# Seven of 128 rows of a row maximum reduced through TensorE, ScalarE and GpSimd instead of VectorE, with 24 loads in place of 29

## The chip, the cores and the metric

One core of one Trainium2 chip runs the program. The metric is the device time of one execution in microseconds; lower is better. Both kernels give the reference's result. A profiled execution gives the span of the program on the core, which is about 1.8 us shorter than the time (kernel before: 163.4 us of 165.17).

## The reference

```python
x = np.random.randn(32, 512, 1024).astype(np.float32)
def reference(x):
    return np.max(x, axis=-1).astype(np.float32)
```

That is 16,384 rows of 1024 floats: 67.1 MB to read and 64 KB to write. Spread over 128 partitions there are 128 rows per partition, and "a row" below means one row in each of the 128 partitions, 512 KB.

## The kernel before

One queue (SyncE) loads several rows at a time into a ring of 45 rows per partition; VectorE reduces each load with one instruction. The loads get smaller towards the end, so that little is left to do when the last one lands; the very last row comes in two halves.

```python
BLOCKS = [
    [14, 13, 12, 11, 9, 8, 8, 7, 6, 5, 5, 4, 4, 3, 3],
    [2, 2, 2, 1, 1, 1, 1, 1, 1, 1, 1, 1],
]
RING = 45
# ... (cut)
        for n in loads:
            if at + n > RING:
                at = 0
            xc = ring[:, at:at + n, :]
            nc.sync.dma_start(out=xc, in_=xb[:, b:b + n, :])
            reduce = nc.vector.reduce_max(out=res[:, first + b:first + b + n], in_=xc, axis=X)
            at += n
            b += n
# ... (cut)
    nc.sync.dma_start(out=half, in_=xb[:, b, :H])
    nc.sync.dma_start(out=tail[:, PAD:], in_=xb[:, b, H:])
    nc.vector.reduce_max(out=tail[:, PAD - 1:PAD], in_=half, axis=X)
    nc.vector.reduce_max(out=res[:, I - 1:], in_=tail[:, PAD - 1:], axis=X)
```

## Time and profile before

| | before |
|---|---|
| time, median (lowest to highest) | 165.0 us (164.85 to 165.12) |
| span of the profiled execution | 163.4 us |
| VectorE busy | 139.0 us, 85% |
| load queue, share of 16 DMA engines' time | 96.6% |
| loads | 27 and two halves |
| last half row landed (landing records) | 159.75 us |

Two shares near the top do not say which of the two, loads or VectorE, sets the end. For that one compares two times: when the last load has landed, and when VectorE gets to it. The prediction below does this with the profile's lines. The trace records 16 landings for each load (496 for the 29 loads and the two stores), taken here as one for each of the page's 16 DMA engines. For each of the five loads that VectorE waited for, its reduction starts 0.02 to 0.03 us behind the last of the 16 (first load: the last landing at 20.29 us, the reduction at 20.31).

### The profile page before, as it was taken

To read this page: it belongs to the slowest core of one execution; us is meant where nothing else is said; L and a number is where in the kernel's file an instruction comes from. 1 tells how busy PE (TensorE), PEld (TensorE's weight loads), DVE (VectorE), ACT (ScalarE), POOL (GpSimd) and SP (SyncE) were. 2 spreads that over 40 slices of the span, in tenths; PEclk is the share of its full clock that TensorE was granted. 3 is DMA by queue.
4 is the path that set the end of the run, shared out by engine and by line. 5 is a ranking of instruction groups with operands and counts; after the bars stand their busy time and mean duration, and the time that the engine had idled before them with its cause. 6 is when DMAs were issued, how large, how long until landed. Compare 5 with 4: busy or idle time off the path is not lost.

```text
span 163.4 us, 117 instructions
## 1 busy us (share of the span) xinstructions
DVE 139.0 (85%) x29; POOL 0.2 (0%) x4
## 2 busy tenths in 40 slices
DVE  0000099989998999999999999999999999999994
POOL 0000000000000000000000000000000000000000
DMA  6999999999989989999989999999999999999990
GB/s 225 449 449 449 433 417 417 417 401 529 433 385 430 452 386 432 433 433 441 457 385 481 401 442 422 409 438 421 446 409 425 437 410 422 427 407 409 409 355 16
DMA packets 4464, 67.18 MB, mean 411 GB/s; under 512 B 752, under 2 KB 752, under 8 KB 2160
## 3 DMA queue, kind: packets, MB, share of 16 engines
q1 hardware_dynamic: 4176, 67.11, 96.6%
q10 hardware_dynamic: 288, 0.07, 0.2%
HBM read 67.11 MB, written 0.07 MB: 411 GB/s over the span
## 4 chain that ended last, share of the span: by engine, by line
DVE 49%; DMA 48%; SPq 1%; issue 0%
DMA ring<-in_x_dram 48%; DVE res L58 48%; SPq L57 1%; DVE res L70 0%; DVE tail L69 0%
## 5 line engine op out<-in xcount | busy, mean ns | idle before, releaser
L58 DVE TENSOR_REDUCE res<-ring 128x1 f32<-128x1024 f32 (+12 forms) x27 | 137.7, 5165 | 22.1 <-DMA ring<-in_x_dram 22.1
L70 DVE TENSOR_REDUCE res<-tail 128x1 f32<-128x513 f32 x1 | 0.7, 686 | 0.0
L69 DVE TENSOR_REDUCE tail<-ring 128x1 f32<-128x512 f32 x1 | 0.7, 682 | 0.0
L90 POOL MEMSET const-bfloat16-1.0<- 128x1 bf16 x1 | 0.1, 102 | 0.0
L90 POOL MEMSET const-uint8-127<- 128x1 uint8 x1 | 0.1, 102 | 0.0
L90 POOL MEMSET const-float32-0.0<- 128x1 f32 x1 | 0.1, 99 | 0.2 <-issue 0.2
L90 POOL MEMSET const-float32-1.0<- 128x1 f32 x1 | 0.1, 99 | 0.0
## 6 DMA issues: line engine op xcount, KB each, us to landing
ring<-in_x_dram SPq DMA_DIRECT2D x2, 4096.0 KB, 25.6
ring<-in_x_dram SPq DMA_DIRECT2D x1, 7168.0 KB, 19.6
ring<-in_x_dram SPq DMA_DIRECT2D x1, 6656.0 KB, 34.9
ring<-in_x_dram SPq DMA_DIRECT2D x1, 6144.0 KB, 48.9
ring<-in_x_dram SPq DMA_DIRECT2D x1, 5632.0 KB, 28.5
ring<-in_x_dram SPq DMA_DIRECT2D x2, 2560.0 KB, 38.4
ring<-in_x_dram SPq DMA_DIRECT2D x1, 4608.0 KB, 24.7
ring<-in_x_dram SPq DMA_DIRECT2D x9, 512.0 KB, 13.8
```

The lines of the kernel that those rows point to most:

```text
L57: nc.sync.dma_start(out=xc, in_=xb[:, b:b + n, :])
L58: reduce = nc.vector.reduce_max(out=res[:, first + b:first + b + n], in_=xc, axis=X)
L69: nc.vector.reduce_max(out=tail[:, PAD - 1:PAD], in_=half, axis=X)
L70: nc.vector.reduce_max(out=res[:, I - 1:], in_=tail[:, PAD - 1:], axis=X)
L90: nc = _bacc.Bacc("TRN2", target_bir_lowering=False, num_devices=1)
```

## The change

The intent is to relieve VectorE. Seven rows, out of the loads numbered 6, 7 and 9 (counted from 0), take a side path: TensorE turns a row in eight 128x128 transposes, ScalarE copies it from PSUM, where the kernel has TensorE write it, GpSimd takes the maximum over partitions, eight small transposes bring the maxima back, and VectorE merges the eight values of each row. With VectorE relieved, the loads can be larger and fewer. The identity that TensorE needs is made by VectorE.

```diff
 BLOCKS = [
-    [14, 13, 12, 11, 9, 8, 8, 7, 6, 5, 5, 4, 4, 3, 3],
+    [15, 15, 15, 15, 14, 11, 11, 8, 4, 4],
     [2, 2, 2, 1, 1, 1, 1, 1, 1, 1, 1, 1],
 ]
+TENSOR = {
+    6: [("turn", 6, 0), ("turn", 6, 1), ("back", 6, 0), ("back", 6, 1)],
+    7: [("turn", 7, 0), ("turn", 7, 1), ("turn", 7, 2), ("back", 7, 0), ("back", 7, 1)],
+    9: [("turn", 9, 0), ("turn", 9, 1), ("back", 7, 2), ("back", 9, 0), ("back", 9, 1)],
+}
+BY_GPSIMD = {6: 2, 7: 3, 9: 2}
+MERGE = {8: 6, 12: 7, 16: 9}
 # ... (cut: pools, the identity)
+    def turn(j, k):
+        rows, cols = tiles[j]
+        ps = psum.tile([P, D], F32)
+        for c in range(C):
+            in_turn("PE", nc.tensor.transpose(
+                out=ps[:, c * P:(c + 1) * P],
+                in_=rows[:, k, c * P:(c + 1) * P],
+                identity=ident,
+            ))
+        sb = turned.tile([P, D], F32)
+        nc.scalar.copy(out=sb, in_=ps)
+        top = allr.tile([P, D], F32)
+        nc.gpsimd.partition_all_reduce(top, sb, P, bass_isa.ReduceOp.max)
+        tops[j, k] = top
+
+    def back(j, k):
+        if j not in backs:
+            fetched = psmall.tile([P, BY_GPSIMD[j], C], F32)
+            backs[j] = fetched
+        for c in range(C):
+            in_turn("PE", nc.tensor.transpose(
+                out=backs[j][:, k, c:c + 1],
+                in_=tops[j, k][0:1, c * P:(c + 1) * P],
+                identity=ident[0:1, 0:1],
+            ))
 # ... (cut)
-            reduce = nc.vector.reduce_max(out=res[:, first + b:first + b + n], in_=xc, axis=X)
+            m = BY_GPSIMD.get(j, 0)
+            tiles[j] = xc[:, n - m:, :], cols[:, n - m:]
+            for what, i, k in TENSOR.get(j, []):
+                (turn if what == "turn" else back)(i, k)
+            reduce = in_turn("DVE", nc.vector.reduce_max(
+                out=cols[:, :n - m], in_=xc[:, :n - m, :], axis=X))
+            if j in MERGE:
+                i = MERGE[j]
+                in_turn("DVE", nc.vector.reduce_max(out=tiles[i][1], in_=backs[i], axis=X))
```

More of the change, by code (lines that the diff above doesn't have):

```diff
@@ L4 @@
 import concourse.tile as tile
-from concourse import bass_utils, mybir
+from concourse import bass_isa, bass_utils, mybir
 from concourse._compat import with_exitstack
@@ L17 @@
 RING = 45
+TENSOR = {
[5 more added lines that the diff above has]
+MERGE = {8: 6, 12: 7, 16: 9}
+NOSYNC = mybir.DependencyInfo(mybir.DependencyClass.NoSync, mybir.DependencyReason.DATA)
 SYNC = mybir.DependencyInfo(mybir.DependencyClass.Sync, mybir.DependencyReason.DATA)
@@ L30 @@
     X = mybir.AxisListType.X
+    ALU = mybir.AluOpType
     xf = x.flatten_outer_dims()
@@ L34 @@
     H = D // 2
+    C = D // P
     I = N // P
@@ L38 @@
     once = ctx.enter_context(tc.tile_pool(name="once", bufs=1))
+    turned = ctx.enter_context(tc.tile_pool(name="turned", bufs=2))
+    allr = ctx.enter_context(tc.tile_pool(name="allr", bufs=2))
+    psum = ctx.enter_context(tc.tile_pool(name="psum", bufs=3, space=bass.MemoryType.PSUM))
+    psmall = ctx.enter_context(tc.tile_pool(name="psmall", bufs=2, space=bass.MemoryType.PSUM))
     ring = once.tile([P, RING, D], F32)
@@ L43, with in_turn @@
     tail = once.tile([P, PAD + H], F32)
-    at = first = 0
+    latest = {}
+    def in_turn(engine, inst):
+        if engine in latest:
+            tc.add_manual_dep(inst.ins, latest[engine].ins.name, NOSYNC, reason="in turn")
+        latest[engine] = inst
+        return inst
+    ident = once.tile([P, P], F32)
+    colno = once.tile([P, P], F32)
+    rowno = once.tile([P, 32], F32)
+    in_turn("DVE", nc.vector.memset(ident, 1.0))
+    in_turn("DVE", nc.vector.memset(rowno, 0.0))
+    in_turn("DVE", nc.vector.tensor_tensor_scan(
+        out=colno, data0=ident, data1=ident, initial=-1.0, op0=ALU.add, op1=ALU.mult))
+    in_turn("DVE", nc.vector.transpose(out=rowno, in_=colno[:, :32]))
+    for q in range(1, P // 32):
+        part = rowno[q * 32:(q + 1) * 32, 0:1]
+        in_turn("DVE", nc.vector.tensor_scalar(
+            out=part, in0=part, scalar1=float(q * 32), scalar2=None, op0=ALU.add))
+    in_turn("DVE", nc.vector.tensor_scalar(
+        out=ident, in0=colno, scalar1=rowno[:, 0:1], scalar2=None, op0=ALU.is_equal))
+    tiles = {}
+    tops = {}
+    backs = {}
+    def turn(j, k):
[22 more added lines that the diff above has]
+            ))
+    at = first = j = 0
     views = []
@@ L57 @@
             nc.sync.dma_start(out=xc, in_=xb[:, b:b + n, :])
-            reduce = nc.vector.reduce_max(out=res[:, first + b:first + b + n], in_=xc, axis=X)
+            cols = res[:, first + b:first + b + n]
+            m = BY_GPSIMD.get(j, 0)
[7 more added lines that the diff above has]
+                in_turn("DVE", nc.vector.reduce_max(out=tiles[i][1], in_=backs[i], axis=X))
             at += n
             b += n
+            j += 1
         first += S
@@ L68 @@
     nc.sync.dma_start(out=tail[:, PAD:], in_=xb[:, b, H:])
-    nc.vector.reduce_max(out=tail[:, PAD - 1:PAD], in_=half, axis=X)
-    nc.vector.reduce_max(out=res[:, I - 1:], in_=tail[:, PAD - 1:], axis=X)
+    in_turn("DVE", nc.vector.reduce_max(out=tail[:, PAD - 1:PAD], in_=half, axis=X))
+    in_turn("DVE", nc.vector.reduce_max(out=res[:, I - 1:], in_=tail[:, PAD - 1:], axis=X))
     store = nc.scalar.dma_start(out=views[0][0], in_=views[0][1])
```

## The prediction

> **What bounds the kernel now.** I read the page of the profile first, then the timeline of VectorE and of the load queue, then the groups by form, then the table of stretches. From the page:
>
> ```profile
> span 163.4 us, 117 instructions
> ...
> DVE 139.0 (85%) x29; POOL 0.2 (0%) x4
> ...
> q1 hardware_dynamic: 4176, 67.11, 96.6%
> ...
> DVE 49%; DMA 48%; SPq 1%; issue 0%
> ```
>
> VectorE is busy for 85% of the span, but the load queue fills 96.6% of it. The chain that ended last is half one, half the other, so the question is which of them the end belongs to. The timeline (start, duration, engine, line) answers it:
>
> ```profile
> 20.31 15.09 DVE L58 TENSOR_REDUCE res<-ring 128x14 f32<-128x14336 f32 x1 [20.31 <-DMA ring<-in_x_dram]
> 36.05 14.02 DVE L58 TENSOR_REDUCE res<-ring 128x13 f32<-128x13312 f32 x1 [0.65 <-DMA ring<-in_x_dram]
> 50.58 12.95 DVE L58 TENSOR_REDUCE res<-ring 128x12 f32<-128x12288 f32 x1 [0.51 <-DMA ring<-in_x_dram]
> ...
> 94.27 65.48 DVE L58 TENSOR_REDUCE res<-ring 128x8 f32<-128x8192 f32 x21 [0.21 <-DMA ring<-in_x_dram]
> ...
> 150.77 0.33 SPq L68 DMA_DIRECT2D tail<-in_x_dram  x1
> 159.66 0.68 DVE L69 TENSOR_REDUCE tail<-ring 128x1 f32<-128x512 f32 x1
> ...
> 160.38 0.69 DVE L70 TENSOR_REDUCE res<-tail 128x1 f32<-128x513 f32 x1
> 161.10 0.34 ACTq L75 DMA_DIRECT2D out_dram<-res  x1
> ```
>
> VectorE has no gap from 94.27 us on, so it looks like the bound. The last load says otherwise:
>
> ```profile
> tail<-in_x_dram SPq DMA_DIRECT2D x1, 256.0 KB, 9.0
> ```
>
> Issued at 150.77 and landed 9.0 us later, the last half row is there at 159.8 (159.75 in the landing records). VectorE begins to reduce it at 160.38, only 0.6 us late. So the loads own the end; VectorE adds 0.6 us of backlog and its last 0.7 us reduction.
>
> **Cost of a load.** The first three lines of the timeline start at landings: 13 rows take 36.05 - 20.31 = 15.74 us, 12 rows 14.53 us, so about 1.21 us a row (a row is 512 KB). Single rows are slower, as the table of stretches shows (last column GB/s):
>
> ```profile
> 1.60:50.00 48.40, 29.04 (x2) 0.00 (x0) 1.00 1.02 435
> 148.20:157.10 8.90, 8.90 (x8) 0.00 (x0) 1.00 1.03 411
> ```
>
> 524,288 bytes at 411 GB/s are 1.276 us. Both fit 1.206 us a row plus 0.07 us a load (12 rows: 14.54).
>
> **Cost of a reduction.** By form:
>
> ```profile
> L58 DVE TENSOR_REDUCE res<-ring 128x14 f32<-128x14336 f32 x1 | 15.1, 15086 | 20.3 <-DMA ring<-in_x_dram 20.3
> L58 DVE TENSOR_REDUCE res<-ring 128x13 f32<-128x13312 f32 x1 | 14.0, 14019 | 0.7 <-DMA ring<-in_x_dram 0.7
> ```
>
> 15,086 - 14,019 = 1,067 ns a row. The unbroken 65.48 us hold 60 rows in 21 instructions: 60 x 1.067 = 64.0, leaving 0.07 us an instruction. A single row thus costs 1.13 us against 1.28 us of its load: VectorE catches up 0.15 us with each.
>
> [...]
>
> **The change, part by part.**
>
> 1. *Fewer, larger loads.* 29 loads become 24 for the same 128 rows: 5 x 0.07 = 0.35 us less. Last landing about 159.4 us instead of 159.75.
>
> 2. *A later start.* The first load has 15 rows, not 14: VectorE starts 1.2 us later, at 21.5. This is harmless, as parts 3 and 4 show.
>
> 3. *Ring.* Three loads of 15 fill its 45 rows. The fourth needs the first one's reduction, at 21.5 + 16.1 = 37.6, while loads two and three keep the queue busy until 21.5 + 2 x 18.16 = 57.8. The fifth is issued at 39.7 + 16.1 = 55.8, the sixth at 57.8 + 16.1 = 74, before load four lands at 76. So at least one whole load is queued behind the running one at every refill, and no gap comes. The rows sent round VectorE lie in slots never loaded again, so a slow GpSimd doesn't hold up a load.
>
> 4. *VectorE loses seven rows,* 7 x 1.067 = 7.5 us. These can't come off the end, which the loads own. With landings from part 1, VectorE waits for nearly every load; its lag at the end of the two-row loads is one reduction. Landings: load 6 (eleven rows) 119.6, load 7 129.4, load 8 134.3, load 9 139.2, the last two-row load 146.6, the ninth single row 158.1. Three merges of 16 or 24 values are added (estimate 0.15 us each). From 148.8 us: merge 0.15, four single rows 4.5, merge 0.15, ready at about 153.6; five more rows end at 159.3 (the last waits for 158.1), first half 159.9, second half 160.6. Before it was 161.07: **0.5 us less**.
>
> 5. *The side path.* A turn is eight transposes[...], a copy of 1024 elements[...], then GpSimd's t, then eight small transposes back[...].[...] TensorE's order is part of this: the turns of load 7 stand behind the way back of load 6, so there GpSimd idles for one turn.
>
>    I do not know t. I chose about 3 us because the program's order makes sense there: both ways back of load 6 stand before load 7's turns, which costs nothing only if two reductions take no longer than load 7 needs to land, and the third way back of load 7 stands behind load 9's turns, as if it were expected about then.
>
> 6. *Preparation.* The identity takes seven or eight small VectorE instructions in the 21 us it idles anyway: no cost. [...]a few more instructions are fetched. I allow 0.2 us, on the load queue or at the ends.
>
> Sum: -0.5 (VectorE's end, the 0.35 of fewer loads contained in it) + 0.2 = -0.3 in the fitting case. To that comes about 0.2 us as the share of the cases in which the side path is somewhat late. 165.0 - 0.3 + 0.2 = 164.9; I place the single figure at **164.7**, nearer the fitting case.
>
> **Rivals.** *A wait for GpSimd takes the place of the wait for loads:* [...]the end follows the seven reductions at 7 us for each us of t. Nothing in the profile measures it; against it stands the order of the program[...].[...] *Expected gain through freed VectorE:* who takes 85% busy and the unbroken 65 us for the bound expects 7 us less, 158. The landing of the last half row at 159.75 speaks against it: the loads alone do not end before 159.4. *Other traffic delays the loads:* all 16 DMA engines are full (96.6%), so every byte of [...]instructions fetched on one of them puts off the end by its own time[...]. *Same ends:* all fits, 164.3 to 164.7.
>
> **Range and chances.** The fitting case and its small delays cover 164.2 to 165.2. A moderate delay[...] reaches 167. Range 164.0 to 167.2. A gain of 2% (below 161.7) would need the loads to end 3 us earlier[...]: 0.01. A loss of 2% (above 168.3)[...]: 0.11. Within 2%: 0.88.
>
> **What would show it.** Right: the last half row lands at 159.4 +- 0.3; VectorE busy about 132 us with idle time <- DMA spread over nearly all loads; final reduction starts within 0.1 us of the half before it; no VectorE wait <- TensorE at the merges. Wrong: a wait of VectorE <- PE before the second or third merge[...]; starts of GpSimd's reductions more than 4 us apart; landings of single rows over 1.28 us apart, or later than 159.8 (then traffic was added); load-queue share falling well below 96% (then the ring starved).

Where a cut is marked, the text had times for a turn, a copy and a way back of the side path, the time table and the limits for t (GpSimd's time for one reduction) made from them, a library of GpSimd and an example of its size, a limit for the rate of the loads. The sum came to -0.5 + 0.2 = -0.3 us in the fitting case, to 164.9 us with 0.2 us added for a late side path, and the single figure was put at 164.7. That the loads themselves can gain little rests on the queue's 96.6% and on the 435 GB/s of the first stretch.

## The result, and the profile after

The changed kernel takes 165.83 us (165.78 to 165.94, four runs) against 165.0 us before. The ratio is 1.0051, with a 95% interval of 1.0034 to 1.0069. Ratios here are the mean time of one kernel's fast runs over that of the other's fast runs of the same rounds, so they are not quite the ratio of the medians.

The page of the changed kernel, same parts as shown of before, with two more lines from the parts on DMA and on the costliest groups:

```profile
span 164.0 us, 368 instructions
...
q1 hardware_dynamic: 3456, 67.11, 95.9%
...
q8 instruction: 1, 0.02, 0.0%
...
DMA 69%; DVE 28%; SPq 1%; issue 0%
...
L106 POOL PARTITION_ALL_REDUCE top<-sb x7 | 22.5, 3269 | 127.2 <-ACT sb L104 127.2
L104 ACT COPY sb<-ps 128x1024 f32<-128x1024 f32 x7 | 7.1, 1013 | 136.2 <-PE ps L98 134.5
```

The chain that ended last has gone over to the loads: 69% DMA, where before it was shared half and half. VectorE really was relieved: it is busy for 134.0 us, before 139.0. GpSimd's reduction takes 3.27 us by its record; in the timeline (start, duration) two of them in a row take 6.43 us, so they follow each other every 3.2 us:

```profile
119.39 3.65 PE L98 MATMUL ps<-ident,ring 128*128 128x128 f32 x16 [119.39 <-DMA ring<-in_x_dram]
...
122.47 6.43 POOL L106 PARTITION_ALL_REDUCE top<-sb  x2 [122.05 <-ACT sb L104]
...
150.14 1.01 PE L115 MATMUL fetched<-ident,top 1*128 1x1 f32 x8 [2.20 <-POOL top L106]
...
153.81 0.16 DVE L143 TENSOR_REDUCE res<-fetched 128x2 f32<-128x16 f32 x1
...
160.20 0.68 DVE L155 TENSOR_REDUCE tail<-ring 128x1 f32<-128x512 f32 x1
160.91 0.69 DVE L156 TENSOR_REDUCE res<-tail 128x1 f32<-128x513 f32 x1
```

The last maxima are back at 151.2 us, and VectorE merges them at 153.8 without an idle mark in brackets: nobody waits for the side path. Yet the final reduction starts at 160.91, 0.5 us later than before (160.38).

Why the loads are late shows in one line of the page, easily overlooked: "q8 instruction: 1", one transfer of 0.02 MB of instructions in the middle of the stream. The record of this transfer says one packet of 16,384 bytes, start 146.31 us, 1,079 ns. The 16 landing times of the loads around it (from the landing records, us, sorted; the middle ones cut) tell what it did:

```
third two-row load     145.89 145.90 145.92 ... 146.15 146.16 146.21 146.22
first single row       147.16 147.18 147.19 ... 147.43 147.46 147.49 148.81
second single row      148.43 148.44 148.47 ... 148.69 148.71 148.76 150.10
last half row          158.73 158.74 158.76 ... 158.97 159.00 159.03 160.32
```

Up to 146.2 us the 16 landings lie within 0.4 us for every load. From the first single row on, one of them is 1.3 us behind the other 15, and it stays so to the end. (The trace does not name the engine of the transfer; that one engine has the transfer and the late landings is read from the times.) On the other 15 the loads are not late; the last half row would be complete at 159.03 (159.15 in the run with one transpose back of eight, which has no transfer), but it is complete at 160.32.

### The profile page after: what moved, and what is told of

The parts are those of the page before. It is cut to its first block, busy times and chain, and to the rows that moved or that the text cites. A ratio compares the mean times of both kernels' runs of the same rounds, so it can differ in the third digit from the quotient of the medians.

```text
span 164.0 us, 368 instructions
## 1 busy us (share of the span) xinstructions
PE 19.1 (12%) x112; PEld 17.6 (11%) x112; DVE 134.0 (82%) x35; ACT 8.4 (5%) x8; POOL 22.7 (14%) x11
## 3 DMA queue, kind: packets, MB, share of 16 engines
q1 hardware_dynamic: 3456, 67.11, 95.9%
## 4 chain that ended last, share of the span: by engine, by line
DMA 69%; DVE 28%; SPq 1%; issue 0%
DMA ring<-in_x_dram 69%; DVE res L139 27%; SPq L133 1%; DVE res L156 0%; DVE tail L155 0%
## 5 line engine op out<-in xcount | busy, mean ns | idle before, releaser
L139 DVE TENSOR_REDUCE res<-ring 128x1 f32<-128x1024 f32 (+7 forms) x22 | 131.0, 5969 | 26.6 <-DMA ring<-in_x_dram 26.1
L106 POOL PARTITION_ALL_REDUCE top<-sb x7 | 22.5, 3269 | 127.2 <-ACT sb L104 127.2
L98 PE MATMUL ps<-ident,ring 128*128 128x128 f32 x56 | 12.6, 421 | 119.4 <-DMA ring<-in_x_dram 119.4
L98 PEld LDWEIGHTS ps<-ident,ring 128*128 128x128 f32 x56 | 11.5, 228 | 119.4 <-issue 119.4
L104 ACT COPY sb<-ps 128x1024 f32<-128x1024 f32 x7 | 7.1, 1013 | 136.2 <-PE ps L98 134.5
L115 PE MATMUL fetched<-ident,top 1*128 1x1 f32 x56 | 6.7, 236 | 12.7 <-POOL top L106 12.7
L115 PEld LDWEIGHTS fetched<-ident,top 1*128 1x128 f32 x56 | 6.1, 203 | 14.0 <-POOL top L106 13.7
L143 DVE TENSOR_REDUCE res<-fetched 128x2 f32<-128x16 f32 (+1 forms) x3 | 0.5, 166 | 0.0
## 6 DMA issues: line engine op xcount, KB each, us to landing
ring<-in_x_dram SPq DMA_DIRECT2D x9, 512.0 KB, 15.2
```

Source lines behind the costliest of these rows:

```text
L98: in_turn("PE", nc.tensor.transpose(out=ps[:, c * P:(c + 1) * P], in_=rows[:, k, c * P:(c + 1) * P], identity=ident,))
L104: nc.scalar.copy(out=sb, in_=ps)
L106: nc.gpsimd.partition_all_reduce(top, sb, P, bass_isa.ReduceOp.max)
L115: in_turn("PE", nc.tensor.transpose(out=backs[j][:, k, c:c + 1], in_=tops[j, k][0:1, c * P:(c + 1) * P], identity=ident[0:1, 0:1],))
L139: reduce = in_turn("DVE", nc.vector.reduce_max(out=cols[:, :n - m], in_=xc[:, :n - m, :], axis=X))
L143: in_turn("DVE", nc.vector.reduce_max(out=tiles[i][1], in_=backs[i], axis=X))
```

## The experiments

Theory A: with more instructions on TensorE, a block of them is fetched during the run, the 16,384 bytes of the record; it occupies one of the 16 DMA engines, which the loads fill to 95.9%, for 1.08 us, and every later load waits for that engine. Rivals: the larger loads themselves (B), VectorE as the bound (C), TensorE's, ScalarE's or GpSimd's reading and writing in SBUF, where the kernel has its ring (D), a library for GpSimd as the thing fetched (E).

| kernel | transposes | instruction transfer, start | last half row landed | time, median |
|---|---|---|---|---|
| before | 0 | none | 159.75 | 165.0 |
| before, seven rows left out | 0 | none | 159.47 | 164.89 |
| new loads, seven rows left out | 0 | none | 159.13 | 164.46 |
| changed, one transpose back of eight | 63 | none | 159.15 | 164.55 |
| changed | 112 | 146.31 | 160.32 | 165.83 |
| changed, no GpSimd | 112 | 144.44 | 160.48 | 166.01 |
| before + 112 idle transposes | 112 | 17.52 | 160.87 | 166.32 |
| before + 336 idle transposes | 336 | 17.43 and 31.12 | 160.83 | 166.29 |
| before + 80 idle transposes | 80 | none | 159.52 | 164.94 (one run) |
| before + 96 idle transposes | 96 | 163.65, after the span (163.3) | 159.48 | 165.04 (one run) |
| new loads, VectorE alone | 0 | none | 159.13 | 170.71 (one run) |
| four rows on the side path, 26 loads | 64 | none | 159.22 | 164.84 |
| changed, ways back in groups | 80 | none | 159.20 | 165.31 |
| the same, last merge later | 80 | none | 159.18 | 164.64 |

(The second, third and fourth columns are from the profiled execution of each, landings from the landing records. The profiled execution of the kernel before took 165.17 us, so its 159.75 is rather late: the three other profiles of the same loads without a transfer in the stream end at 159.47 to 159.52.)

**The side path taken away.** The seven rows are neither reduced nor sent; results are wrong in those columns.

```diff
-TENSOR = {6: [...], 7: [...], 9: [...]}
-MERGE = {8: 6, 12: 7, 16: 9}
+TENSOR = {}
+MERGE = {}
+    in_turn("DVE", nc.vector.memset(res, 0.0))      # in place of the identity
```

> The changed kernel's loads, with the seven rows left out altogether: no TensorE, no ScalarE copy, no GpSimd, no merge (wrong results in seven columns, on purpose). Theory A (the 16 KB instruction fetch on one DMA engine is what the change paid): no fetch in the DMA table, all 16 engines land together again, last half row at 159.3 us instead of 160.3, final reduction starts by 160.1, time 164.4 to 164.8. Theory B (the new loads themselves are the slower part, for instance the 15-row loads): last landing stays at 160.3, time 165.7 to 165.9. Theory C (the seven rows were the bound all along): time below 163.

Measured 164.46 us, ratio to before 0.9973 (0.9958 to 0.9988), last landing 159.13. So the new loads are not the slow part: with 24 of them the kernel is 0.45 us faster than before. Rivals B and C are out, the latter because even with seven rows for nothing the time does not go below 164.

**Fewer transposes back.** Everything stays but seven of the eight small transposes of each row (wrong results).

```diff
-            fetched = psmall.tile([P, BY_GPSIMD[j], C], F32)
+            fetched = psmall.tile([P, BY_GPSIMD[j], 1], F32)
-        for c in range(C):
+        for c in range(1):
```

> The changed kernel with one of the eight transposes back of each row (wrong results in seven columns, on purpose): 63 transposes instead of 112; GpSimd, ScalarE and VectorE do all they did. Theory A (fetch of TensorE's instructions): no 16 KB instruction transfer, last landing 159.3, time 164.5 to 164.9, 1 us less than the changed kernel. Rival D (GpSimd's or TensorE's reading of SBUF slows the loads): landing and time within 0.2 us of the changed kernel's 160.3 and 165.8. Rival E (the fetch belongs to GpSimd's library): the 16 KB transfer stays, and so does the time.

Measured 164.55 us, ratio 0.9978 (0.9961 to 0.9995). The page of this run has no line for an instruction queue, and the queue and timeline lines that answer to those of the changed kernel are:

```profile
span 162.8 us, 270 instructions
...
q1 hardware_dynamic: 3456, 67.11, 96.6%
q10 hardware_dynamic: 288, 0.07, 0.2%
HBM read 67.11 MB, written 0.07 MB: 413 GB/s over the span
...
L106 POOL PARTITION_ALL_REDUCE top<-sb x7 | 22.5, 3267 | 125.8 <-ACT sb L104 125.8
```

```profile
159.73 0.69 DVE L156 TENSOR_REDUCE res<-tail 128x1 f32<-128x513 f32 x1
```

GpSimd still does its seven reductions in 22.5 us, and the span is 1.2 us shorter. Rivals D and E do not fit: all of GpSimd's and ScalarE's work is there, and the loss is gone. Of TensorE's work 49 small transposes are missing, so its part of D is left to the runs with idle transposes below.

**GpSimd taken away, transposes kept.** The ways back read the turned row (wrong results).

```diff
-        top = allr.tile([P, D], F32)
-        nc.gpsimd.partition_all_reduce(top, sb, P, bass_isa.ReduceOp.max)
-        tops[j, k] = top
+        tops[j, k] = sb
```

> The changed kernel with the reduction over partitions left out: the transposes back read the turned row itself (wrong results, on purpose). All 112 transposes stay. Theory A: the 16 KB instruction transfer is still there, though perhaps earlier, one engine ends about 1.3 us after the others, time 165.6 to 165.9. Rivals D (GpSimd's traffic) and E (GpSimd's library): transfer gone or landing at 159.3, time 164.4 to 164.9.

Measured 166.01 us (165.82 to 166.25), 0.1 us over the range I had written, ratio 1.0068 (1.0053 to 1.0083). The transfer is there, at 144.44, 1.9 us earlier; TensorE does not wait for GpSimd here, for which it waited 12.7 us in the changed kernel. GpSimd's reduction is gone and the transfer is not, so the transfer is neither caused by GpSimd's work nor a library for it.

**The transposes put into the kernel before.** VectorE makes the identity as in the change, and TensorE turns a constant tile into PSUM at the start; nothing reads it, and the results are right.

```diff
+    for _ in range(14):
+        ps = psum.tile([P, D], F32)
+        for c in range(D // P):
+            nc.tensor.transpose(out=ps[:, c * P:(c + 1) * P], in_=colno, identity=ident)
```

> The kernel before, with the identity made by VectorE and 112 transposes of a constant tile on TensorE at the start, which nothing reads (results right). Theory A: the 16 KB instruction transfer appears, on one engine, early in the stream; that engine stays about 1.0 to 1.3 us behind to the end, last landing about 160.8 instead of 159.75, time 165.9 to 166.3. Rival: an early delay of one engine is made up over the rest of the stream, or needs the late collision of the changed kernel: time within 0.2 us of 165.0. If TensorE is not whose instructions are fetched, no transfer appears and the time is 165.0.

Measured 166.32 us (166.0 to 166.49), 0.02 us over the expected range, ratio 1.0083 (1.0068 to 1.0098), 1.3 us more than before. This is the loss of the change, alone, in a kernel without any side path:

```profile
q1 hardware_dynamic: 4176, 67.11, 96.0%
q10 hardware_dynamic: 288, 0.07, 0.2%
q8 instruction: 1, 0.02, 0.0%
```

```profile
2.57 13.84 PE L64 MATMUL ps<-ident,colno 128*128 128x128 f32 x112 [2.57 <-DVE ident L59]
21.51 15.09 DVE L79 TENSOR_REDUCE res<-ring 128x14 f32<-128x14336 f32 x1 [18.99 <-DMA ring<-in_x_dram]
```

TensorE is done at 16.4 us, the transfer runs from 17.5 to 18.5 us, and the first load, whose reduction started at 20.31 in the kernel before, is reduced from 21.51 on. 140 us later the lag is still there: the last half row lands at 160.87 instead of 159.75. By the landing records the last engine is 1.34 us behind the next one at the first load and 1.31 us at the last half row: with the load queue at 96.0% it did not catch up. The 112 transposes, all of one constant tile, take 124 ns each (13.84 us).

**Three times as many.** 336 transposes instead of 112, otherwise the same.

> The kernel before with 336 transposes that nothing reads, three times as many as in the run with 112. Theory A: two or three instruction transfers of 16 KB; if they go to the same DMA engine each adds 1.1 us, so two make 167.1 to 167.6 and three 168.2 to 168.7; if each goes to another engine they don't add up and the time stays at 166.0 to 166.6. Rival (it is TensorE's activity or its first use, not the count of its instructions): one transfer or none more, 166.0 to 166.5, with no second step in any engine's landings.

Measured 166.29 us (166.24 to 166.41), ratio 1.0080, and two transfers (the page: "q8 instruction: 2"). The branch of the expectation that came true is that they do not add up. The landing records show why; here the first load and the second:

```
14 rows    19.59 ... 20.02 20.05 21.46
13 rows    35.34 ... 35.77 37.02 37.21
```

After the first transfer one landing of the 16 is late, by 1.4 us; after the second, two are, by 1.25 and 1.44 us, which is read as a second engine that lags. VectorE starts behind the last landing, so two late ones cost no more than one: 166.29 us here, 166.32 with one transfer. That is two transfers only; a third one on either of these engines was not seen.

**How many are too many.** 80 and 96 idle transposes.

> The kernel before with 80 transposes at the start that nothing reads: where between 64 (no transfer seen) and 112 (transfer) does the 16 KB transfer begin? Theory A: transfer and time go together, 165.0 without it, 166.0 to 166.5 with it; and 80 here must agree with the 80 of the grouped kernel, wherever in time its transposes lie.

> The same with 96 transposes. Transfer and a lagging engine together, 166.0 to 166.5, or neither, 165.0. No third outcome fits Theory A.

With 80 there is no transfer and 164.94 us. With 96 the transfer comes at 163.65 us, after the end of the span (163.3 us), where it delays nothing: 165.04 us (one run each). This is a third outcome for which my text had no place: I had expected transfer and lag to go together. The trace counts fit a request at a certain place in TensorE's program: with 96 transposes the whole program has 198 records on TensorE (the page shows 96 weight loads and 96 matmuls for the 96 transposes; six records are start and end), of which 195 were over at 15.2 us without a transfer, and in the changed kernel 198 had started when its transfer began. In the other runs more had started: 214 without GpSimd, 227 with 112 idle transposes, 241 with 336 (491 at the second transfer). So if the place is the same in all runs it is about the 198th record, and the transfer starts 0.4 to 3.0 us after it; this is an inference, and which rule lies behind it the runs do not show.

These two runs also answer the rest of rival D: 80, 96 and 112 idle transposes keep TensorE busy in the same place (until 13.8, 15.2 and 16.4 us) and differ in nothing but their number, and only the run with the transfer in the stream is slow.

**VectorE relieved alone.** The kernel before, with its own loads, leaves seven rows out (wrong results).

```diff
+LEFT_OUT = {6: 2, 7: 3, 9: 2}
-            reduce = nc.vector.reduce_max(out=res[:, first + b:first + b + n], in_=xc, axis=X)
+            m = n - LEFT_OUT.get(j, 0)
+            reduce = nc.vector.reduce_max(out=res[:, first + b:first + b + m], in_=xc[:, :m, :], axis=X)
```

> The kernel before, its own 29 loads, with two, three and two rows of the seventh, eighth and tenth load left unreduced and nothing else added but a memset of the result tile (wrong results in seven columns, on purpose). It measures what 7.5 us less of VectorE is worth alone. Theory A (the loads own the end; the last single row and the two halves behind it cost VectorE about 1.3 us after the last landing whatever went before): last landing 159.7 to 159.8, time 164.7 to 165.0, at most 0.15 us gained. Rival (VectorE's backlog was worth what the prediction gave it beside the loads, 0.15 to 0.5 us): 164.4 to 164.8. Rival C (VectorE was the bound): 158 to 162.

Measured 164.89 us, ratio 0.9995 (0.9979 to 1.0010): 7.5 us less work on the engine that is 85% busy is worth nothing that can be told from zero. The last landing, 159.47, was earlier than the expected 159.7 to 159.8, a range that fits the one profile of the kernel before (159.75) and not the others.

**The new loads alone.** VectorE reduces all 128 rows, with the changed kernel's list of loads in the kernel before.

> The kernel before with the changed kernel's 24 loads, and no side path: VectorE reduces all 128 rows. Theory A: the loads end at 159.2, but VectorE, which starts at 21.3 and waits for the next three loads, cannot catch up: 2 us of waits at loads 2, 3, 4 each, then unbroken, final reduction starting about 165.9, time 170 to 171. So the seven rows pay for the larger loads. Rival: the larger loads alone carry the gain, time 164.4 to 165.

Measured 170.71 us (one run), inside the expected 170 to 171. The loads end at 159.13, but VectorE starts the final reduction only at 165.94. The two halves of the change need each other: without the side path the larger loads cost 5.7 us, without the larger loads seven rows less on VectorE gain nothing.

**Four rows and 26 loads.** A version with fewer transposes, results right: the first block is 15, 14, 15, 13, 12, 9, 10, 7, 8, 3, 3, 3, and four rows of its ninth load take the side path.

> The changed kernel with four rows of one load sent round VectorE instead of seven, and 26 loads instead of 24 (first block 15, 14, 15, 13, 12, 9, 10, 7, 8, 3, 3, 3): 64 transposes instead of 112, results right. Theory A: no instruction transfer, last landing 159.3 to 159.5, final reduction starts by 159.9, time 164.5 to 164.8, below both kernels. If 64 transposes are already enough for a transfer: 165.7 to 166.0. Rival D: 165.3 or more, since TensorE, ScalarE and GpSimd still run.

Measured 164.84 us (164.77 to 165.06, five runs), ratio 0.9995 (0.9982 to 1.0008). There is no transfer and the landing is as expected (159.22), and it is 1 us faster than the changed kernel; but the time is just above my range, and against the kernel before the gain is not clear of zero.

**All seven rows, fewer instructions.** The rows of one load are brought together in partitions 0, 32 and 64 of one tile, and one transpose brings back the same 128 columns of all of them: 24 small transposes instead of 56, 80 in all, results right. (The order of TensorE's work and the number of PSUM buffers change with it; not shown.)

```diff
+        if k == 0:
+            tops[j] = allr.tile([P, D], F32, name="group")
+        top = tops[j] if k == 0 else others.tile([P, D], F32)
         nc.gpsimd.partition_all_reduce(top, sb, P, bass_isa.ReduceOp.max)
+        if k:
+            nc.scalar.copy(out=tops[j][32 * k:32 * k + 1, :], in_=top[32 * k:32 * k + 1, :])
# ... (cut)
+        K = 32 * (BY_GPSIMD[j] - 1) + 1
-                in_=tops[j, k][0:1, c * P:(c + 1) * P],
+                in_=tops[j][:K, c * P:(c + 1) * P],
```

> The changed kernel with all seven rows on the side path and its 24 loads, but 24 transposes back instead of 56: the rows of one load are put in partitions 0, 32 and 64 of one tile (ScalarE copies the second and third), and one transpose brings back the same 128 columns of all of them. 80 transposes in all instead of 112, results right. Theory A, if 80 are few enough for no instruction transfer: last landing 159.2, time 164.4 to 164.8, below both kernels by 0.3 and 1.2 us. Theory A, if 80 are still too many: transfer there, 165.6 to 166.0. Rival D (work of the side path, not its instructions): 165.6 to 166.0 without a transfer.

Measured 165.31 us, ratio 1.0015 (1.0002 to 1.0029), which no branch had. The transfer was gone and the loads ended at 159.20, but the timeline has a new wait, in brackets:

```profile
151.85 1.04 ACT L111 COPY group<-top 1x1024 f32<-1x1024 f32 x1 [5.64 <-POOL top L109]
...
154.04 0.17 DVE L147 TENSOR_REDUCE res<-fetched 128x2 f32<-128x16 f32 x1 [0.78 <-PE fetched L118]
```

The last way back starts 2.8 us later than in the changed kernel: the last extra copy takes 1.04 us, and GpSimd starts on the last two rows at 145.39 instead of 143.65, since ScalarE turns to them only after the extra copy of the rows before. VectorE waits 0.78 us at the last merge. Behind it VectorE runs without a gap to the end, here as in the next run, so the wait goes to the end almost whole: the final reduction starts at 160.48, in the next run at 159.74. This is the first rival of the prediction, in small.

**The last merge later.** One number changes, so that VectorE asks after the sixth single row and not after the fourth.

```diff
-MERGE = {8: 6, 12: 7, 16: 9}
+MERGE = {8: 6, 12: 7, 18: 9}
```

> The grouped kernel (80 transposes, results right) with its last merge after the sixth single-row reduction instead of the fourth, about 2.3 us later. In the grouped run there was no transfer and the loads ended at 159.20, but VectorE waited 0.8 us for the last merge. Theory A: no wait for TensorE at the merge, final reduction starting at 159.7 to 159.8, time 164.4 to 164.7, below both kernels. Rival: what costs the grouped kernel is not the wait for the merge (extra ScalarE copies, say), time stays at 165.2 to 165.4.

Measured 164.64 us (164.51 to 164.69, five runs), ratio to before 0.9976 (0.9962 to 0.9989): the fastest kernel with right results here, 0.4 us below the kernel before and 1.2 us below the changed one.

```profile
155.42 0.17 DVE L147 TENSOR_REDUCE res<-fetched 128x2 f32<-128x16 f32 x1
...
159.74 0.69 DVE L160 TENSOR_REDUCE res<-tail 128x1 f32<-128x513 f32 x1
```

No wait at the merge, and the final reduction 1.2 us before that of the changed kernel (160.91).

## Why the prediction was right or wrong

The class (within 2%) and the range (164.0 to 167.2) held. The single figure of 164.7 did not: the kernel is slower than before by 0.5%, not faster by 0.2%. The range held because it left room up to 167 for a moderate delay, not because this loss had been worked out. Point by point:

- *What bounds the kernel.* Right. Leaving out seven of 128 rows on VectorE alone moved the ratio to 0.9995.
- *Part 1, fewer loads.* Right. On the engines that land first, which no transfer disturbs, the last half row comes at 159.12 before and at 158.70 with the new loads, 0.42 us less against 0.35 predicted. The last of the 16 engines gained 0.6 us between those two profiles; the spread of the 16 engines differs by 0.2 us between profiles (0.63 us in that of before, 0.38 us in that of the same loads with seven rows left out). Over the table's profiles without a transfer in the stream the old loads end at 159.47 to 159.75, the 24 new ones at 159.13 to 159.20.
- *Part 2, the later start, and part 3, the ring.* Right: no gap in the loads.
- *Part 4, VectorE.* Right in direction, and its share was as small as the sum implied. Without the transfer VectorE ends 1.27 us after the last landing (159.73 + 0.69 against 159.15); before, 1.32 us (160.38 + 0.69 against 159.75). The gain is almost all from the loads. One detail was wrong and cost nothing: VectorE did not wait "for nearly every load" but for 8 of the 24 (26.1 us in all, 18.8 of them for the first).
- *Part 5, the side path.* Right, in part by luck: a turn to the start of the copy took 2.0 us, the copy 1.01, the way back 1.01, a merge 0.16 (0.15 estimated), and t 3.2 us ("about 3"). The first three were assumed from figures that no trace of this case had shown, and are cut from the text. GpSimd stood idle for 4.2 us before the rows of load 7, behind the way back of load 6, as the text says. And t was guessed from the order of the program, with no measurement behind it. The side path fitted with 2.7 us to spare (back at 151.2, asked for at 153.8); 0.7 us of this spare is owed to the late loads, since with one transpose back of eight, and no transfer, VectorE asked at 153.1.
- *Part 6, preparation.* **This step failed.** It said "a few more instructions are fetched. I allow 0.2 us, on the load queue or at the ends". The term was mis-sized: the transfer cost 1.2 us, the difference of the last landings with and without it (160.32 and 159.15) and of the times (165.83 and 164.55). The rival "other traffic delays the loads" named what the runs then showed, one of 16 full engines putting off the end, but without a count: I did not count TensorE's instructions, 224 for 112 transposes where there had been none.
- *The signs.* No wait of VectorE for TensorE, as listed under right, and GpSimd's reductions, where one follows on another, 3.2 us apart and not the "more than 4" listed under wrong. Idle time "over nearly all loads" did not come (8 of 24). A last landing "later than 159.8 (then traffic was added)" stood under wrong, and it is what came.
- *"By its own time" in that rival.* By an estimate, a sixteenth of the 433 GB/s of the load of 13 rows (6.8 MB in 15.74 us), 16,384 bytes on one engine would take 0.6 us. Measured were 0.9 to 1.1 us, and a lag of 1.3 to 1.4 us behind the other engines. The loads' own packets of 16,384 bytes did take 0.61 us in the same trace; why the block took longer is not shown.

That the block belongs to TensorE is shown by the runs of the kernel before that differ in nothing but the number of idle transposes: no transfer at 80, after the span at 96, in the stream at 112, two at 336. The other versions agree: none with 63, 64 and 80 transposes, one with 112, with and without GpSimd. The one transfer of the changed kernel is 16,384 bytes by its record, and it shows in the 16 landing times above: of the last half row 15 are there by 159.03, the last at 160.32. That VectorE goes by the last of the 16 shows where it waited: the first single row had 15 landings by 147.49 and the last at 148.81, and its reduction started at 148.83.

What stays open: what decides which of the engines a block comes in on, and at which instruction exactly it is asked for.

## What to carry to other kernels

Where the loads fill the DMA engines to the end, as here (96.6%), count the instructions a change adds, not only their time: with 112 transposes on TensorE in place of none a block of 16,384 bytes of instructions was fetched during the run, and in the loads after it one landing of the 16 was late (1.3 us, whether the block came at 17 us or at 146 us); with 80 no block came, with 96 only after the end. Look for the instruction queue in the DMA table and for one straggler among a load's landings before blaming the new work. And relieving an engine that is 85% busy was worth only what it let the true bound, here the loads, do better: 7.5 us less of VectorE alone gave a ratio of 0.9995, with the larger loads 0.9973.
